# Attention keys ordered by column, values stored once per row range and loaded once per four tiles, q and keys in one request each

## The chip, the cores and the metric

The kernel runs on one NeuronCore of one Trainium2 chip. The metric is the device time of one execution in microseconds (us); smaller is better. Engines are called as in the profile: PE (TensorE), PEld (its weight loads), DVE (VectorE), ACT (ScalarE), POOL (GpSimd) and SP (SyncE, which here only issues DMA requests). DMA requests are issued by SP and by ACT, and sixteen DMA engines move the bytes.

## The reference, cut to what matters

One layer over 2048 latent tokens (a grid of 32 rows by 64 columns) and 256 context tokens, model width 1024, in f32. A combined projection feeds two head groups; the change touches the first, neighbourhood attention with 8 heads of width 64.

```
h_lat = rmsnorm(x) * (1 + scale) + shift ;  h_ctx likewise
na_q, na_k, na_v, na_g, r_q, r_k, r_v, r_g = split(h @ w_in)
# group A: each query reads an 8 x 16 window of the grid and all 256 context keys, in one softmax
s_loc = q . k[window] * 64**-0.5 + bias ;  s_ctx = q . k_ctx * 64**-0.5
p = softmax(concat(s_loc, s_ctx)) ;  o_na = p_loc @ v[window] + p_ctx @ v_ctx
# group B: retention in chunks of 128, forward and backward (r_q, r_k, r_v)
y = concat(o_na * silu(na_g), headnorm(o_ret) * silu(r_g)) @ w_out
out = rmsnorm(x + gate * y)
```

## The kernel before, in words

**Stages.** The projection comes first: the normed inputs are split into a high and a low f32r part, and every product is made of three matmuls (high by high, low by high, high by low). Projected q, k, v and gates go to DRAM (`qS`, `kS`, `vS`, `gS` and others). Then comes attention over 128 tiles, with further projection work woven in between as filler for PE (`fill`). The retention scans and the output projection end the program.

**Storing values.** `u_v` makes the values of 256 tokens and two head pairs into a tile `o` (a ring of two buffers) and stores it with one request on ACT's queue into `vS`, which is ordered by token. `jobs` lists the units of the projection in order; after each unit `tick` issues the stores that were put off by one unit, and `spill_step` issues one request of 512 KB on SP (`hS`).

**Attention tiles.** Head `h` has 16 tiles: four row ranges `i` by four column ranges `j`. A tile has 128 queries (8 rows by 16 columns). `KWIN[i]` gives the rows of its keys, (first, count), `CWIN[j]` the columns:

```
KWIN = [(0, 12), (4, 16), (12, 16), (20, 12)]
CWIN = [(0, 24), (8, 32), (24, 32), (40, 24)]
```

So a tile has 288, 384 or 512 grid keys and 256 context keys. The loop over `t` runs these steps, each some tiles behind the one before: `s_mm` (line 748) multiplies q by the grid keys, read straight out of the head's key tile `k2`, and by the context keys; `s_min`, `s_exp` and `s_norm` make the softmax on DVE, ACT and POOL; `p_tr` transposes the probabilities in groups of keys; `pv` (line 796) multiplies them by the values `vt`; `combine` adds the parts. The order of instructions on each engine is the order in which this loop writes them, so PE does nothing else while an `s_mm` waits for its q.

**Loads in attention.** All are on SP's queue, in program order. `load_head` brings a head's keys with two requests (high and low half of `k2`, 64 partitions each), and the context values `vc`; it runs at tile (1, 2) of the head before. `load_q` brings the queries of a row range with two requests of the same 64 rows, one to each half of the partitions; the ring `q` has two buffers, and the load for row range `i + 1` is issued at tile (i, 0), four tiles ahead. `load_v` brings four grid rows of values with four requests, one per column range, into a ring of six. `bias` brings a tile's bias (`nb`), `load_gate` a gate (`gt`). Each DMA request of SP or ACT takes the next of eight completion counters (DMAHW0 to DMAHW7 in the instruction lists), in turn, and waits until the last request on the same counter has landed.

Of the kernel before, what the change touches and what calls it, by code (L numbers as in the profile page):

```python
# [9 lines left out]
F32 = mybir.dt.float32  # L10
# [8 lines left out]
P = 128  # L19
D = 1024  # L20
KC = D // P
L = 2048
# [58 lines left out]
def hybrid_kernel(ctx: ExitStack, tc: tile.TileContext, a: dict, out: bass.AP):  # L81
# [63 lines left out]
    def store(dst, src, n=1):  # L145
        q = env["queue"]
        defer(n, lambda: q.dma_start(dst, src))
# [268 lines left out]
    def u_v(w, c0, tp):  # L416
        pm = yield from tokform(w, tp)
        vt = op.tile([P, 2, 2, 2, P], F32R, name="o")
        pv = pm.rearrange("p (t h e d) -> p t h e d", t=2, h=2, e=2)
        for e in range(2):  # L420
            hs, ls = slice(64 * e, 64 * e + 64), slice(64 - 64 * e, 128 - 64 * e)
            nc.scalar.copy(vt[:, :, :, e, hs], pv[:, :, :, e, :])
            nc.vector.tensor_tensor(vt[:, :, :, e, ls], pv[:, :, :, e, :], f(vt)[:, :, :, e, hs], ALU.subtract)
        store(vS[(c0 - 1024) // WG][tp * 256:(tp + 1) * 256].rearrange("(t p) h d -> p t (h d)", p=P),
              f(vt).rearrange("p t h e d -> p t (h e d)"))
# [279 lines left out]

    def load_head(h):
        k2 = kp.tile([P, LT], F32R, name="k2")
        for hl in range(2):
            nc.sync.dma_start(f(k2)[64 * hl:64 * hl + 64, :], kS[h // 2][64 * (h % 2):64 * (h % 2) + 64, hl, :])
        vh = vS[h // 4][:, h % 4, :]  # L710
        vc = kp.tile([P, 2, P], F32R, name="vc")
        nc.sync.dma_start(f(vc), vh[L:, :].rearrange("(n p) d -> p n d", p=P))
        return dict(k2=k2, vh=vh, vc=vc, vt={}, q={})

    def load_q(hd, h, i):
        q = kp.tile([P, 2, 512], F32R, name="q", bufs=2)
        src = qS[h // 2][i, 64 * (h % 2):64 * (h % 2) + 64]
        for e in range(2):
            nc.sync.dma_start(f(q)[64 * e:64 * e + 64], src)
        hd["q"][i] = q  # L720

    def load_v(hd, gs):
        for g in gs:
            vt = kp.tile([P, 4, P], F32R, name="vt", bufs=6)
            src = hd["vh"][4 * g * GW:(4 * g + 4) * GW, :].rearrange("(r c) d -> r c d", c=GW)
            for j, (c0, cw) in enumerate(CWIN):
                nc.sync.dma_start(f(vt)[:4 * cw, j, :], src[:, c0:c0 + cw, :])
            hd["vt"][g] = vt

    def bias(h, rt, ct):  # L730
        n, o = BT[rt][ct]
# [8 lines left out]
    def s_mm(t):  # L740
        h, i, j, kr0, kr, kc0, cw = dims(t)
        hd, nk, odd = heads[h], kr * cw, t % 2
        pl = sS[:, 1024:1024 + nk] if odd else sS[:, 512 - nk:512]
        pc = sS[:, 768:1024] if odd else sS[:, 512:768]
        kg = hd["k2"][:, :L].rearrange("p (r c) -> p r c", c=GW)
        for o, k in ((pl, kg[:, kr0:kr0 + kr, kc0:kc0 + cw]), (pc, hd["k2"][:, L:])):
            for hl in range(2):
                nc.tensor.matmul(o, hd["q"][i][:, hl, j * P:(j + 1) * P], k, start=(hl == 0), stop=(hl == 1))  # L748
        tl_st[t] = dict(s=sS[:, 768:1024 + nk] if odd else sS[:, 512 - nk:768], nk=nk, lo=LC * odd, co=nk * (1 - odd),
                        sp=ap_.tile([P, 768], F32, name="sp", bufs=3), st=ap_.tile([P, 4], F32, name="stt", bufs=4))  # L750
# [19 lines left out]
    def p_tr(t):  # L770
        h, i, j, kr0, kr, kc0, cw = dims(t)
        T = tl_st[t]
        sp, nk, ng_, cn = T["sp"], T["nk"], kr // 4, 4 * cw
# [13 lines left out]
    def pv(t):  # L787
        h, i, j, kr0, kr, kc0, cw = dims(t)
        T, hd = tl_st[t], heads[h]
        pt, ng_ = T["pt"], T["ng"]  # L790
        if t % 2 == 0:
            tl_st["po"] = psc.tile([P, 2, 2, P], F32, name="po")
        po = tl_st["po"]
        cn = 4 * cw
        for g in range(ng_):
            nc.tensor.matmul(po[:, t % 2, :, :], hd["vt"][kr0 // 4 + g][:cn, j, :], pt[:cn, g, :, :], start=(g == 0), stop=False)  # L796
# [37 lines left out]

    heads[0] = load_head(0)
    load_q(heads[0], 0, 0)
    load_v(heads[0], (0, 1, 2))
    for n in range(4):
        run(n)
        if n == 0:  # L840
# [116 lines left out]
    for t in range(NT + 3):  # L957
# [34 lines left out]
            load_gate(t)  # L992
        if i < 3 and j == 0:
            load_q(hd, h, i + 1)
        for g in {(0, 2): (3,), (0, 3): (4,), (1, 1): (5,), (1, 3): (6,), (2, 3): (7,)}.get((i, j), ()):
            load_v(hd, (g,))
        if h + 1 < NH:
            if i == 1 and j == 2:
                heads[h + 1] = load_head(h + 1)
            if i == 3:  # L1000
                nh = heads[h + 1]
                if j == 0:
                    load_q(nh, h + 1, 0)
                    bias(h + 1, 0, 0)
                    load_v(nh, (0,))
                if j == 2:
                    bias(h + 1, 0, 1)
                if j == 3:
                    bias(h + 1, 0, 2)
                    load_v(nh, (1, 2))  # L1010
# [295 lines left out]
def _bias_rows(rpb):  # L1306
# [4 lines left out]
    out = []  # L1311
    for i in (0, 1, 3):
        r = qr + 8 * i
        k = np.arange(KWIN[i][1]).reshape(1, -1, 1) + KWIN[i][0]
        lo = np.clip(r - 4, 0, GROWS - 8)
        for j in (0, 1, 3):
            c = qc + 16 * j
            m = np.arange(CWIN[j][1]).reshape(1, 1, -1) + CWIN[j][0]
# [27 lines left out]
```

## Time and profile before

| | |
|---|---|
| time of the three runs shown | 1433.92 us median (1433.7 to 1440.09) |
| the profiled execution | 1431.96 us, span 1430.0 us |
| PE busy | 1351.1 us, 94% of the span |
| DVE, ACT, POOL busy | 641.0, 531.0, 495.0 us |
| TensorE clock granted, mean | 0.986 |
| bytes moved by DMA | 264.14 MB |
| first and last `s_mm` matmul | 561.4 and 1072.9 us from the span's start |

Rows of the view by groups read "line engine operation, tile written <- tiles read, shape, count, then busy us, mean ns of one, idle time before them and what ended it". Waits read "who waited <- for whom: us in total, times, longest". Rows of stretches give each engine's busy us, the granted clock, the mean busy share of the sixteen DMA engines and GB/s. Of a DMA request, size and count are shown; the little packets of 4 bytes by which DMA engines report that they have finished are counted under "under 512 B".

### The profile page before, as it was taken

The page shows a single profiled execution, that of the slowest core. Times are in us where ns is not written, and L with a number is a line of the kernel's source. Part 1 is how long each engine was busy: PE and PEld are TensorE (multiplying, and loading weights), DVE is VectorE, ACT ScalarE, POOL GpSimd, SP SyncE. Part 2 cuts the span into 40 slices and gives each one's busy share as a digit, 9 for nine tenths or more (in the row PEclk, how much of TensorE's full clock was granted, in tenths as well). Part 3 has the DMA queues.
Part 4 walks back from the last instruction along what each step waited for, and adds up shares of the span by engine and source line. Part 5 has one row for each costly group of instructions (what it writes and reads, how often), then busy time and mean ns, then how long its engine had stood idle before and what let it go on. Part 6 is the DMA issues. An engine that isn't in the chain of part 4 may idle for free.

```text
span 1430.0 us, 22693 instructions
## 1 busy us (share of the span) xinstructions
PE 1351.1 (94%) x8380; PEld 1179.9 (83%) x8380; DVE 641.0 (45%) x1244; ACT 531.0 (37%) x1155; POOL 495.0 (35%) x499
## 2 busy tenths in 40 slices
PE   7989999999999999999899978798999989999997
PEld 2567899988887888998799877697999779888886
DVE  5786111100021222566666765476564544344445
ACT  5454212212212222655455433345563234333332
POOL 5442302202201221355354432235443144454442
PEclk9999999999999999999999998899999999999999
DMA  9444656223354677767758696867645998555433
GB/s 320 153 162 148 229 196 229 104 88 103 104 169 147 222 259 218 179 179 194 178 160 205 174 236 163 235 172 197 166 138 170 275 316 259 192 177 169 155 119 125
DMA packets 213072, 264.14 MB, mean 185 GB/s; under 512 B 14305, under 2 KB 160865, under 8 KB 211938
## 3 DMA queue, kind: packets, MB, share of 16 engines
q1 hardware_dynamic: 177282, 197.93, 48.1%
q10 hardware_dynamic: 35680, 64.76, 12.7%
q8 instruction: 67, 1.10, 0.3%
q14 instruction: 43, 0.35, 0.1%
HBM read 179.80 MB, written 82.84 MB: 184 GB/s over the span
## 4 chain that ended last, share of the span: by engine, by line
PE 73%; DMA 13%; DVE 7%; issue 2%; ACT 2%; POOL 2%; SPq 1%; ACTq 0%; DVEq 0%; POOLq 0%
PE mm L355 25%; PE mm L366 18%; PE mm L1190 10%; DMA q<-qS 5%; PE sS L748 4%; PE tr L775 2%; PE po L796 2%; DMA vt<-vS 2%; PE mm L915 2%; PE mm L299 2%; PE tr L777 1%; PE po L798 1%; DMA v<-rvS 1%; PE mm L1102 1%; PE mm L1101 1%
## 5 line engine op out<-in xcount | busy, mean ns | idle before, releaser
L355 PE MATMUL mm<-hhi,whi 128*128 128x512 f32 x640 | 260.0, 406 | 0.0
L355 PE MATMUL mm<-hlo,whi 128*128 128x512 f32 x640 | 254.0, 397 | 5.6 <-DVE hlo L268 2.2
L355 PE MATMUL mm<-hhi,wlo 128*128 128x512 f32 x640 | 253.8, 397 | 0.3 <-DVE wlo L336 0.3
L366 PE MATMUL mm<-whi,hhi 128*128 128x256 f32 x768 | 225.0, 293 | 0.0
L366 PE MATMUL mm<-wlo,hhi 128*128 128x256 f32 x768 | 217.3, 283 | 2.6 <-POOL wlo L336 2.6
L366 PE MATMUL mm<-whi,hlo 128*128 128x256 f32 x768 | 216.3, 282 | 0.0
L336 POOL TENSOR_TENSOR wlo<-st,whi 128x256 fp32r<-128x256 f32 (+1 forms) x97 | 112.3, 1175 | 251.1 <-ACT whi L334 250.8
L779 ACT CAST pt<-tr 128x640 fp32r<-128x640 f32 (+1 forms) x128 | 95.6, 747 | 217.9 <-PE tr L777 192.6
L785 DVE TENSOR_TENSOR pt<-tr,pt 128x640 fp32r<-128x640 f32 (+1 forms) x128 | 113.9, 890 | 105.2 <-ACT pt L779 104.6
L768 POOL TENSOR_SCALAR sp<-sp,stt 128x640 f32<-128x640 f32 (+2 forms) x128 | 103.7, 811 | 136.0 <-DVE stt L767 94.9
L366 PEld LDWEIGHTS mm<-wlo,hhi 128*128 128x128 f32 x768 | 145.4, 189 | 3.3 <-POOL wlo L336 3.2
L355 PEld LDWEIGHTS mm<-hlo,whi 128*128 128x128 f32 x640 | 121.0, 189 | 31.4 <-issue 3.2
L366 PEld LDWEIGHTS mm<-whi,hlo 128*128 128x128 f32 x768 | 145.7, 190 | 0.0
L366 PEld LDWEIGHTS mm<-whi,hhi 128*128 128x128 f32 x768 | 145.7, 190 | 0.0
L355 PEld LDWEIGHTS mm<-hhi,wlo 128*128 128x128 f32 x640 | 120.7, 189 | 29.5 <-DVE wlo L336 0.7
L355 PEld LDWEIGHTS mm<-hhi,whi 128*128 128x128 f32 x640 | 121.0, 189 | 28.5 <-issue 4.6
L757 DVE CUSTOM_DVE_ANT_0 sp<-sS,nb 128x640 f32<-128x640 f32 (+2 forms) x128 | 105.6, 825 | 53.4 <-PE sS L748 43.0
L748 PE MATMUL sS<-k,q 128*128 128x256 f32 (+3 forms) x512 | 101.7, 321 | 27.3 <-DMA q<-qS 21.8
L748 PEld LDWEIGHTS sS<-k,q 128*128 128x128 f32 x512 | 85.1, 192 | 36.5 <-issue 19.9
L762 ACT ACTIVATE sp<-sp,stt 128x640 f32<-128x640 f32 (+2 forms) x128 | 107.5, 839 | 20.1 <-DVE stt L757 19.8
L1190 PE MATMUL mm<-wor,y 128*128 128x512 f32 x384 | 95.6, 398 | 1.3 <-DVE xt L1199 1.2
L1190 PE MATMUL mm<-won,y 128*128 128x512 f32 x336 | 89.9, 406 | 0.0
(214 smaller groups left out, 2238.8 us busy)
## 6 DMA issues: line engine op xcount, KB each, us to landing
st<-in_w_in_dram SPq DMA_DIRECT2D x48, 512.0 KB
q<-qS SPq DMA_DIRECT2D x64, 256.0 KB
vS<-o ACTq DMA_DIRECT2D x18, 512.0 KB
k<-kS SPq DMA_DIRECT2D x16, 576.0 KB
kS<-o SPq DMA_DIRECT2D x16, 512.0 KB
woS<-g ACTq DMA_DIRECT2D x32, 256.0 KB
qS<-o ACTq DMA_DIRECT2D x16, 512.0 KB
vt<-vS SPq DMA_DIRECT2D x128, 64.0 KB
```

The source lines that it names most:

```text
L299: nc.tensor.matmul(aps[u][0:s.shape[2], :], s[:, 2 * j + k, :], w, start=(j == 0 and i == 0 and k == 0), stop=(j == 3 and i + 1 == len(ops ...
L336: eng.tensor_tensor(l, r, f(h), ALU.subtract)
L355: nc.tensor.matmul(pm[:, :n], ww[:, k, cs], h[:, k, :], start=(k == 0 and i == 0), stop=(k == KC - 1 and i == 2))
L366: nc.tensor.matmul(pm[:, t * WG:(t + 1) * WG], h[:, k, o:o + P], ww[:, k, :], start=(k == 0 and i == 0), stop=(k == KC - 1 and i == 2))
L748: nc.tensor.matmul(o, hd["q"][i][:, hl, j * P:(j + 1) * P], k, start=(hl == 0), stop=(hl == 1))
L757: nc.vector.tensor_tensor_reduce(T["sp"][:, :n], T["s"], nbz[big][:, o:o + n], -1.0, 3e38, ALU.add, ALU.min, T["st"][:, 0:1])
L762: nc.scalar.activation(sp[:, :n], sp[:, :n], AF.Exp, bias=st[:, 0:1], scale=-1.0, accum_out=st[:, 1:2])
L768: nc.gpsimd.tensor_scalar(sp[:, :n], sp[:, :n], st[:, 2:3], 0.0, ALU.mult, ALU.add)
L775: nc.tensor.transpose(tr[:cn, g, :], sp[:, T["lo"] + g * cn:T["lo"] + (g + 1) * cn], ident)
L779: nc.scalar.copy(pt[:, :ng_ + 2, 0, :], tr[:, :ng_ + 2, :])
L785: nc.vector.tensor_tensor(pt[:, :n, 1, :], tr[:, :n, :], f(pt)[:, :n, 0, :], ALU.subtract)
L1190: nc.tensor.matmul(pm, yy[:, k, :], ww[:, k, sl], start=(k == 0 and i == 0), stop=(k == 3 and i == 2))
```

## The change

Keys of a tile are taken column by column instead of row by row (`"p r c -> p c r"` in `s_mm`, and the same in the table of biases), so a transposed group is 8 columns by all rows of the row range, instead of 4 rows by all columns of the column range. Group sizes stay 96 or 128, and the number of groups over a head stays the same. The values of grid tokens are stored to `vB`, one tensor per row range with the partition order (column in a block of 8, row), so that one request of 96 or 128 partitions by 8 blocks brings what all four tiles of a row range need. A row that lies in two row ranges is stored twice; each store is one row of 64 tokens, on SP's queue. `load_q` and `load_head` make one request each, with the two halves as the outermost dimension of the DRAM side. Bias loads move one tile later. The two value jobs stand apart in `jobs`, a gate job between them.

```
-    vS = [dram.tile([LT, 4, P], F32, name=f"vS{t}") for t in range(2)]
+    vS = [dram.tile([LC, 4, P], F32, name=f"vS{t}") for t in range(2)]
+    vB = [[dram.tile([P, 8, 4 * P], F32, name=f"vB{t}_{i}") for i in range(4)] for t in range(2)]
...
+        if tp == 8:
+            store(vS[s].rearrange("(t p) h d -> p t (h d)", p=P), o)
+            return
+        for r in range(4 * tp, 4 * tp + 4):
+            for i, (kr0, kr) in enumerate(KWIN):
+                if kr0 <= r < kr0 + kr:
+                    dst = vB[s][i][:8 * kr].rearrange("(c r) b d -> r b c d", r=kr)[r - kr0]
+                    defer(1, lambda dst=dst, src=o[64 * (r % 2):64 * (r % 2) + 64, r % 4 // 2, :]: nc.sync.dma_start(dst, src))
...
-    jobs = [(1024, [(u_v, (tp,)) for tp in range(9)]), (1280, [(u_v, (tp,)) for tp in range(9)])]
-    jobs += [(c0, [(u_gate, (ct, b)) for ct in range(2) for b in range(4)]) for c0 in (1536, 1792)]
+    jobs = []
+    for e in range(2):
+        jobs += [(1024 + 256 * e, [(u_v, (tp,)) for tp in range(9)]), (1536 + 256 * e, [(u_gate, (ct, b)) for ct in range(2) for b in range(4)])]
...
-        for hl in range(2):
-            nc.sync.dma_start(f(k2)[64 * hl:64 * hl + 64, :], kS[h // 2][64 * (h % 2):64 * (h % 2) + 64, hl, :])
+        nc.sync.dma_start(f(k2), kS[h // 2][64 * (h % 2):64 * (h % 2) + 64].rearrange("p e t -> e p t"))
...
-        for e in range(2):
-            nc.sync.dma_start(f(q)[64 * e:64 * e + 64], src)
+        nc.sync.dma_start(f(q).rearrange("p e t -> p (e t)"), src.rearrange("p e t -> p (e t)").unsqueeze(0).to_broadcast([2, 64, 1024]))
...
-    def load_v(hd, gs):
-        for g in gs:
-            vt = kp.tile([P, 4, P], F32R, name="vt", bufs=6)
-            src = hd["vh"][4 * g * GW:(4 * g + 4) * GW, :].rearrange("(r c) d -> r c d", c=GW)
-            for j, (c0, cw) in enumerate(CWIN):
-                nc.sync.dma_start(f(vt)[:4 * cw, j, :], src[:, c0:c0 + cw, :])
-            hd["vt"][g] = vt
+    def load_v(h, i):
+        vt, n = kp.tile([P, 8, P], F32R, name="vt", bufs=3), 8 * KWIN[i][1]
+        nc.sync.dma_start(f(vt)[:n], vB[h // 4][i][:n, :, (h % 4) * P:(h % 4 + 1) * P])
+        heads[h]["vt"][i] = vt
...
-        for o, k in ((pl, kg[:, kr0:kr0 + kr, kc0:kc0 + cw]), (pc, hd["k2"][:, L:])):
+        for o, k in ((pl, kg[:, kr0:kr0 + kr, kc0:kc0 + cw].rearrange("p r c -> p c r")), (pc, hd["k2"][:, L:])):
...
-        for g in {(0, 2): (3,), (0, 3): (4,), (1, 1): (5,), (1, 3): (6,), (2, 3): (7,)}.get((i, j), ()):
-            load_v(hd, (g,))
+        if j == 3 and 3 < t < NT - 8:
+            load_v((t + 8) // 16, (t + 8) // 4 % 4)
```

What SP issues from tile (1, 2) of head 0 on, when the keys of head 1 are fetched (k, vc), before the change; `q` is the load for row range 3 of head 0, and the numbers behind a name only tell buffers apart:

```order
L709 DMA k_4452<-kS_61 64x2304 [waits DMAHW7_49]
L709 DMA k_4452<-kS_61 64x2304 [waits DMAHW0_49]
L712 DMA vc<-vS_65 128x2x128 [waits DMAHW1_49]
L727 DMA vt<-vS_65 96x1x128 [waits DMAHW3_49,PE_49]
L727 DMA vt<-vS_65 128x1x128 [waits DMAHW5_49]
L727 DMA vt<-vS_65 128x1x128 [waits DMAHW6_49]
L727 DMA vt<-vS_65 96x1x128 [waits DMAHW7_49]
L732 DMA nb_3984<-in_rpb_t_dram 128x288 [waits DMAHW0_49,DVE_49]
L719 DMA q<-qS_57 64x1024 [waits DMAHW1_49,PE_49]
L719 DMA q<-qS_57 64x1024 [waits DMAHW2_49]
```

The same place after the change:

```order
L717 DMA k_4531<-kS_61 128x1x2304 [waits DMAHW6_49]
L719 DMA vc<-vS_65 128x2x128 [waits DMAHW7_49]
L730 DMA vt<-vB_3_70 96x8x128 [waits DMAHW0_49,PE_49]
L735 DMA nb_4088<-in_rpb_t_dram 128x288 [waits DMAHW1_49,DVE_49]
L725 DMA q<-qS_57 128x1x1024 [waits DMAHW2_49,PE_49]
L735 DMA nb_4088<-in_rpb_t_dram 128x384 [waits DMAHW3_49,DVE_49]
L812 DMA gt<-gS_75 64x512 [waits DMAHW4_49,Pool_49]
L735 DMA nb_4088<-in_rpb_t_dram 128x288 [waits DMAHW6_49,DVE_49]
```

Two requests for keys, two for queries and four for values have become one each. The last `nb` of this piece uses the counter of `k` (DMAHW6), so it is issued when `k` has landed; `q` stands ahead of it.

One head later, again on SP after the change, the keys of head 2 and then the queries for row range 3 of head 1:

```order
L717 DMA k_5296<-kS_62 128x1x2304 [waits DMAHW3_49]
L719 DMA vc<-vS_65 128x2x128 [waits DMAHW4_49]
L730 DMA vt<-vB_3_70 96x8x128 [waits DMAHW6_49,PE_49]
L404 DMA rot<-in_rot_c_dram 128x512 [waits DMAHW7_49,DVE_49]
L404 DMA rot<-in_rot_s_dram 128x512 [waits DMAHW1_49,DVE_49]
L735 DMA nb_4088<-in_rpb_t_dram 128x288 [waits DMAHW2_49]
L725 DMA q<-qS_57 128x1x1024 [waits DMAHW3_49,PE_49]
```

Here `q` itself has come onto the counter of `k` (DMAHW3), since fewer requests lie between them.

In the projection, SP before the change issues only the spills and weight loads at the first value job (`st` is the raw weights):

```order
L173 DMA st<-in_w_in_dram 128x4x256 x2
L527 DMA hS_0_85<-hhi 128x1024 x4
L527 DMA hS_1_86<-hlo 128x1024 x4
L527 DMA hS_0_87<-hhi 128x1024
L173 DMA st<-in_w_in_dram 128x4x256 x2
```

After the change the stores of rows lie between the spills:

```order
L174 DMA st<-in_w_in_dram 128x4x256 x2
L433 DMA vB_0_67<-o 8x8x512 x4
L536 DMA hS_0_93<-hhi 128x1024
L433 DMA vB_0_67<-o 8x8x512
L433 DMA vB_1_68<-o 8x8x512
```

The 16 stores of grid values have left ACT's queue, and 112 row stores stand on SP's.

More of the change, by code (lines that the diff above doesn't have):

```diff
@@ L423, in u_v @@
             nc.vector.tensor_tensor(vt[:, :, :, e, ls], pv[:, :, :, e, :], f(vt)[:, :, :, e, hs], ALU.subtract)
-        store(vS[(c0 - 1024) // WG][tp * 256:(tp + 1) * 256].rearrange("(t p) h d -> p t (h d)", p=P),
-              f(vt).rearrange("p t h e d -> p t (h e d)"))
+        s, o = (c0 - 1024) // WG, f(vt).rearrange("p t h e d -> p t (h e d)")
+        if tp == 8:
[6 more added lines that the diff above has]
+                    defer(1, lambda dst=dst, src=o[64 * (r % 2):64 * (r % 2) + 64, r % 4 // 2, :]: nc.sync.dma_start(dst, src))
     def put_tok(dstt, c0, tp, r, n=1):
@@ L707, in load_head @@
         k2 = kp.tile([P, LT], F32R, name="k2")
-        for hl in range(2):
-            nc.sync.dma_start(f(k2)[64 * hl:64 * hl + 64, :], kS[h // 2][64 * (h % 2):64 * (h % 2) + 64, hl, :])
-        vh = vS[h // 4][:, h % 4, :]
+        nc.sync.dma_start(f(k2), kS[h // 2][64 * (h % 2):64 * (h % 2) + 64].rearrange("p e t -> e p t"))
         vc = kp.tile([P, 2, P], F32R, name="vc")
-        nc.sync.dma_start(f(vc), vh[L:, :].rearrange("(n p) d -> p n d", p=P))
-        return dict(k2=k2, vh=vh, vc=vc, vt={}, q={})
+        nc.sync.dma_start(f(vc), vS[h // 4][:, h % 4, :].rearrange("(n p) d -> p n d", p=P))
+        return dict(k2=k2, vc=vc, vt={}, q={})
     def load_q(hd, h, i):
@@ L772, in p_tr @@
         T = tl_st[t]
-        sp, nk, ng_, cn = T["sp"], T["nk"], kr // 4, 4 * cw
+        sp, nk, ng_, cn = T["sp"], T["nk"], cw // 8, 8 * kr
         for g in range(ng_):
@@ L793, in pv @@
         po = tl_st["po"]
-        cn = 4 * cw
+        cn = 8 * kr
         for g in range(ng_):
-            nc.tensor.matmul(po[:, t % 2, :, :], hd["vt"][kr0 // 4 + g][:cn, j, :], pt[:cn, g, :, :], start=(g == 0), stop=False)
+            nc.tensor.matmul(po[:, t % 2, :, :], hd["vt"][i][:cn, kc0 // 8 + g, :], pt[:cn, g, :, :], start=(g == 0), stop=False)
         for g in range(2):
@@ L836, in hybrid_kernel @@
     load_q(heads[0], 0, 0)
-    load_v(heads[0], (0, 1, 2))
+    for i in range(3):
+        load_v(0, i)
     for n in range(4):
@@ L1003, in hybrid_kernel @@
                     load_q(nh, h + 1, 0)
+                if j == 1:
                     bias(h + 1, 0, 0)
-                    load_v(nh, (0,))
-                if j == 2:
+                if j == 3:
                     bias(h + 1, 0, 1)
-                if j == 3:
-                    bias(h + 1, 0, 2)
-                    load_v(nh, (1, 2))
+        if h > 0 and (i, j) == (0, 0):
+            bias(h, 0, 2)
     def load_y(lo, kind, t):
@@ L1313, in _bias_rows @@
         r = qr + 8 * i
-        k = np.arange(KWIN[i][1]).reshape(1, -1, 1) + KWIN[i][0]
+        k = np.arange(KWIN[i][1]).reshape(1, 1, -1) + KWIN[i][0]
         lo = np.clip(r - 4, 0, GROWS - 8)
@@ L1317, in _bias_rows @@
             c = qc + 16 * j
-            m = np.arange(CWIN[j][1]).reshape(1, 1, -1) + CWIN[j][0]
+            m = np.arange(CWIN[j][1]).reshape(1, -1, 1) + CWIN[j][0]
             lc = np.clip(c - 8, 0, GW - 16)
```

## The prediction

> **What bounds the kernel now.** I read the page first, then who waits for whom on PE, then the stretches, then the DMA views.
>
> ```profile
> span 1430.0 us, 22693 instructions
> PE 1351.1 (94%) x8380; PEld 1179.9 (83%) x8380; DVE 641.0 (45%) x1244; ACT 531.0 (37%) x1155; POOL 495.0 (35%) x499
> DMA packets 213072, 264.14 MB, mean 185 GB/s; under 512 B 14305, under 2 KB 160865, under 8 KB 211938
> ```
>
> PE is the bound: 79 us of the span are all that it is not busy. Where those lie, and what the attention stage (first to last tile, 561 to 1085 us) looks like as a whole:
>
> ```profile
> PE sS L748 <- DMA q<-qS: 21.8, 7, 6.6
> PE mm L299 <- ACT o L286: 9.7, 1, 9.7
> PE po L796 <- DMA vt<-vS: 7.0, 2, 3.9
> ...
> PE sS L748 <- DMA vt<-vS: 1.0, 1, 1.0
> ```
>
> ```profile
> core 0: us, PE busy (x) PEld busy (x) DVE busy (x) ACT busy (x) POOL busy (x), PEclk, DMA share, GB/s
> 200.00:220.00 20.00, 20.00 (x171) 20.00 (x170) 3.07 (x8) 4.12 (x9) 0.38 (x1) 1.00 0.27 100
> 561.00:1085.00 524.00, 481.73 (x3551) 454.53 (x3550) 324.95 (x726) 261.48 (x546) 218.86 (x247) 0.97 0.69 182
> 1160.00:1180.00 20.00, 20.00 (x103) 16.75 (x102) 6.67 (x12) 7.40 (x18) 12.85 (x18) 1.00 1.08 346
> ```
>
> In attention PE idles 42 us of 524, 30 of them for q and values, and the clock is 0.97. That is all that quicker loads could bring. A row range (four tiles) takes 524/32 = 16.4 us now, 481.73/32 = 15.1 us of it PE work. The DMA engines are at 0.69 of their time there: transfers, not PE, are what the change moves, so the question is how each new request is carried.
>
> **How a request is spread.** The requests and their sizes (KB each), and a stretch just before attention in which value requests alone move data:
>
> ```profile
> st<-in_w_in_dram SPq DMA_DIRECT2D x48, 512.0 KB
> q<-qS SPq DMA_DIRECT2D x64, 256.0 KB
> ...
> k<-kS SPq DMA_DIRECT2D x16, 576.0 KB
> ...
> qS<-o ACTq DMA_DIRECT2D x16, 512.0 KB
> vt<-vS SPq DMA_DIRECT2D x128, 64.0 KB
> ...
> vt<-vS SPq DMA_DIRECT2D x128, 48.0 KB
> ...
> rg<-in_ret_g_t_dram SPq DMA_DIRECT2D x1, 2.0 KB
> ```
>
> ```profile
> DMA  1222322111000000000011113211223322222111
> GB/s 47 64 70 82 94 82 64 41 47 29 18 12 0 0 0 0 0 0 0 23 47 47 47 41 94 88 47 59 76 82 88 94 76 88 82 70 59 59 53 41
> DMA packets 355, 0.18 MB, mean 50 GB/s; under 512 B 12, under 2 KB 355, under 8 KB 355
> ```
>
> The second fence is 549 to 552.5 us: six requests are issued, all packets are those of 512 B of `vt`, and the DMA share never passes 3 tenths; 94 GB/s is the most. An ordinary stretch (543 to 553 us, with qS stores in it) reaches 9 tenths and 430 GB/s:
>
> ```profile
> DMA  7998989799854423999992101210000122222179
> GB/s 145 221 203 213 295 213 262 279 397 430 330 205 172 152 94 133 389 424 387 426 393 82 55 29 59 86 53 29 0 0 8 45 74 61 82 84 72 49 297 360
> ```
>
> So `vt` runs on about a quarter of the engines. What is special about it is its DRAM side: four grid rows outermost (`src[:, c0:c0+cw]`, 4 x cw x 128), where the others have 64 or more outermost. The completion packets agree. The listing of issues (65 groups, the first and the last shown above) sums to 1,039 requests; at 16 reports each that is 16,624, but the page has only 14,305 packets under 512 B in all. 256 `vt` requests with 4 reports instead of 16 are 3,072 fewer, 13,552, which fits; in the short stretch there are 12 small packets, three finished requests at 4.
>
> I therefore take it that a request runs on as many engines as its outermost count allows. The new `load_q` has `to_broadcast([2, 64, 1024])` and the new `load_head` has `"p e t -> e p t"`: two outermost. Both then run on two engines, where two requests of 64 rows ran on sixteen.
>
> [...]
>
> **The change, part by part.**
>
> *q and keys on two engines.* Rate of one engine: 430/16 = 26.9 GB/s at the peak above, 94/4 = 23.5 in the `vt` stretch, 346/(16 x 1.08) = 20.0 in the row 1160 to 1180 with all engines loaded. I take 25.2, between the first two, since only two engines will be loaded and the rest lightly. Bytes in the stage: 182 GB/s x 524 us = 95.4 MB. Of these q is 31 x 512 KB = 16.3 MB, k is 7 x 1152 KB = 8.3 MB, and 70.9 MB are other requests. After the change each of the two engines carries half of q and k, 12.3 MB, and a sixteenth of the rest, 4.4 MB: 16.7 MB, which at 25.2 GB/s takes 662 us (621 at 26.9, 834 at 20.0). The stage cannot be shorter than that, and it is 524 now.
>
> In one head: a q takes 262 KB/25.2 = 10.4 us, the keys 590 KB/25.2 = 23.4 us, the others 4.4 MB/25.2/32 = 5.5 us a row range. In an ordinary row range q is issued at its start and lands at the fixed time + 10.4 + most of 5.5, about 17 us later: just longer than the 15.1 us of PE work. The keys are issued in the middle of row range 1 and stand ahead of the q for range 3, so range 2 lasts until both are through, about 40 us: `s_mm` of tile (3, 0) should wait some 25 us in seven heads. The fixed time shows at the program's start:
>
> ```profile
> 0.72 0.41 SPq L455 DMA_DIRECT2D silc<-in_c_dram  x1
> 2.42 0.21 ACT L456 ACTIVATE silc<-silc 128x16 f32<-128x16 f32 x1 [0.42 <-DMA silc<-in_c_dram]
> ```
>
> 8 KB are there 1.7 us after issue. In the three ordinary ranges of each head nothing of q is queued for that time: 24 x 1.7 = 41 us (0 if other requests fill it all). Stage: 662 + 41 = 703 us.
>
> *The first head.* Keys are asked for at 530.5 us and the first `s_mm` runs at 561.4:
>
> ```profile
> L709 SPq DMA_DIRECT2D k<-kS x16: 480/592/1285, 530.5 to 978.7; - x16
> L748 PE MATMUL sS<-k,q x512: 274/291/660, 561.4 to 1072.9; 128*128 128x256 f32 x86, 128*128 128x384 f32 x44, 128*128 128x512 f32 x21, 128*128 128x288 f32 x20
> ```
>
> 530.5 + 1.7 + 23.4 + 10.4 + 1.7 = 567.7, and up to six qS stores on the same engines, 33 KB or 1.3 us each, make 575: 7 to 14 us late, I take 10.
>
> *Values loaded once.* 256 requests become 32, of 96 or 128 outermost on both sides, the same bytes on all engines; the two `vt` waits (7.0 and 1.0 us) go, and 224 issues leave SP. The ring of three gives each load eight tiles. None of it shortens a stage that q sets: 0. What SP saves was not on the path either:
>
> ```profile
> L727 SPq DMA_DIRECT2D vt<-vS x256: 504/616/1790, 543.5 to 1059.2; - x128
> SPq L727 <- DMA vt<-vS: 22.7, 30, 2.5
> ```
>
> The second line shows SP waiting on completion counters; with q and k late, those waits grow (rival below).
>
> *Values stored by rows.* 112 requests of 128 KB on SP instead of 16 of 512 KB on ACT, 14.7 MB instead of 8.4. A unit of the value job is 48 matmuls at 293 ns, 14 us, and issues up to 8 stores at about 0.6 us (the SP row above), 5 us; `o` has two buffers, so a store has some 14 us to land. The row 200 to 220 has PE at 20.00 of 20 and DMA at 0.27, so this stays covered: 0, at most one late unit in sixteen jobs, 5 us. Its outermost 8 should mean 8 engines, enough for 16 KB each. The price of a matmul is in
>
> ```profile
> L366 PE MATMUL mm<-whi,hhi 128*128 128x256 f32 x768 | 225.0, 293 | 0.0
> L748 PE MATMUL sS<-k,q 128*128 128x384 f32 x128 | 35.0, 355 | 17.1 <-DMA q<-qS 13.3 <-DVE stt L757 1.8 <-DMA vt<-vS 1.0
> L748 PE MATMUL sS<-k,q 128*128 128x512 f32 x64 | 21.4, 416 | 1.0 <-DVE stt L757 0.9
> L748 PE MATMUL sS<-k,q 128*128 128x288 f32 x64 | 14.5, 308 | 9.2 <-DMA q<-qS 8.5 <-DVE stt L757 0.7
> ```
>
> *Keys by column.* The grid-key matmuls (last three rows, 70.9 us) now read elements 64 apart. No row shows such a read by PE; its cost is between 0 and a doubling, 70.9 us. PE work in the stage would be 552.6 us at the worst, below 703, so q covers it: 0 here. Transposes and `pv` keep their counts, and the softmax its sizes: 0. The later biases spare SP waits for DVE: 0.
>
> **Sum**, against the profiled execution's 1432 us (2 us under the median): 1432 - 524 + 703 + 10 = 1621 us.
>
> **The rivals.**
>
> *Everything behind the keys stops.* A request waits for its completion counter, eight requests back; in the third instruction list the q for range 3 waits for the keys' own counter, and ACT's stores take counters too. Then q starts only when the keys have landed, and up to one range of PE work a head, 15.1 us, is no longer covered: 7 x 15.1 = 106 us more, 1727. For it: three requests fewer lie between k and q. Against it: in the head before, q goes out first.
>
> *The loads are quick enough.* The requests are spread over sixteen engines after all, or two are faster than any row shows; then the 30 us of waits and part of the low clock go: I take 24 us off, 1408, faster than before. It decides when two engines do 16.7 MB in the 482 us of PE work, 35 GB/s each, or when the split is four or more. Against it: the peak of 26.9 and the quarter share of `vt`.
>
> *Spread well, but PE pays for the stride.* 1408 + 71 = 1479, slower; it needs the split to be good and a doubled read. [...]
>
> **How the numbers follow.** Two engines carry q and keys, as summed: 0.78, by its bounds 1529 (26.9 GB/s, no gaps, nothing late at the start) to 1795 (20.0 GB/s). Stopped behind the keys: 0.12, inside that range. Quick loads: 0.05. Stride alone: 0.03. No change within 0.5%, which is about what can be measured: 0.02. Faster 0.05, same 0.02, slower 0.93. The range is that of the first two cases, 1525 to 1795.
>
> **What would show it.** PE's wait for `q<-qS` grows from 21.8 us to about 200, its longest from 6.6 to 20 or more, once in each of seven heads at tile (3, 0); packets under 512 B fall below 16 a request; the DMA share of the stage falls from 0.69 to about 0.5 while PE waits; waits for `vt` vanish; the projection before 530 us keeps its time. I am wrong if the wait for q falls, or if `sS` matmuls lengthen and the stage does not.

## The result, and the profile after

The changed kernel takes 1676.17 us (median of 4 runs, 1674.84 to 1681.17) against 1433.81 us (4 runs, 1430.14 to 1440.09) on the same chip: a ratio of 1.169, 95% interval 1.164 to 1.174. The forecast was 1621, range 1525 to 1795, slower.

The page after, in the lines that were shown of before: span, busy time, packets.

```profile
span 1673.0 us, 22622 instructions
PE 1435.6 (86%) x8380; PEld 1216.5 (73%) x8380; DVE 643.3 (38%) x1244; ACT 531.9 (32%) x1155; POOL 494.1 (30%) x499
DMA packets 215072, 270.43 MB, mean 162 GB/s; under 512 B 13233, under 2 KB 159793, under 8 KB 213938
```

PE does the same 8380 matmuls, is busy 84 us longer and idle 237 us instead of 79. The requests (KB each) and who waits for whom on PE (us in total, times, longest):

```profile
q<-qS SPq DMA_DIRECT2D x32, 512.0 KB
vB<-o SPq DMA_DIRECT2D x112, 128.0 KB
k<-kS SPq DMA_DIRECT2D x8, 1152.0 KB
...
vt<-vB SPq DMA_DIRECT2D x16, 512.0 KB
```

```profile
PE sS L751 <- DMA q<-qS: 116.5, 8, 25.5
PE tr L778 <- DVE pt L788: 52.3, 4, 20.0
PE sS L751 <- DVE stt L760: 18.1, 6, 7.0
PE mm L300 <- ACT o L287: 11.1, 1, 11.1
PE mm L356 <- ACT whi L335: 8.9, 1, 8.9
```

The wait for `q` has grown from 21.8 to 116.5 us and none for `vt` is left on PE. Two others are new: transposes that wait for the softmax (`pt`), 52.3 us, and 8.9 us in the projection (L356). Stretch by stretch, cut at the first score matmul (587.1 us; it was at 561.4) and at 1326, where before has 1085:

```profile
0.00:587.00 587.00, 541.78 (x2844) 439.95 (x2844) 155.94 (x236) 153.00 (x239) 133.88 (x94) 0.98 0.53 178
587.00:1326.00 739.00, 561.43 (x3557) 487.83 (x3558) 328.83 (x727) 262.48 (x547) 220.72 (x248) 0.86 0.42 131
1326.00:1673.00 347.00, 332.40 (x1981) 288.76 (x1980) 158.55 (x281) 116.47 (x369) 139.51 (x158) 0.98 0.63 199
```

The projection is 26 us longer (587 for 561), attention 215 (739 for 524), the rest 2: the 243 us between the spans. In attention the DMA engines are busy 0.42 of their time, 0.69 before, and the granted clock is 0.86. A stretch of attention in 40 slices, 812 to 850 us:

```profile
DMA  1127111110111011152016889711138911114699
GB/s 33 52 99 254 56 63 47 50 69 39 47 58 67 39 58 58 58 144 89 36 42 144 258 222 302 184 61 52 52 91 265 249 55 52 49 46 105 190 325 310
```

For long runs of slices one tenth of the engines is busy and some 50 GB/s move, which reads as two engines of sixteen at 25 GB/s each; in 21.7 of the 38 us the trace has exactly two packets under way. In these slices the keys, and then a `q`, are on their way, and next to nothing else moves.

### The profile page after: what moved, and what is told of

Its sections match the earlier page's. It is cut to its first block, busy times and chain, and to the rows that moved or that the text cites. A ratio compares the mean times of both kernels' runs of the same rounds, so it can differ in the third digit from the quotient of the medians.

```text
span 1673.0 us, 22622 instructions
## 1 busy us (share of the span) xinstructions
PE 1435.6 (86%) x8380; PEld 1216.5 (73%) x8380; DVE 643.3 (38%) x1244; ACT 531.9 (32%) x1155; POOL 494.1 (30%) x499
## 2 busy tenths in 40 slices
DMA packets 215072, 270.43 MB, mean 162 GB/s; under 512 B 13233, under 2 KB 159793, under 8 KB 213938
## 4 chain that ended last, share of the span: by engine, by line
PE 61%; DMA 22%; SPq 7%; DVE 4%; issue 3%; POOL 1%; ACT 1%; ACTq 0%; DVEq 0%; POOLq 0%
PE mm L356 21%; PE mm L367 13%; PE mm L1194 9%; DMA q<-qS 7%; PE sS L751 5%; DMA k<-kS 5%; SPq L735 4%; DMA nb<-in_rpb_t_dram 4%; SPq L730 2%; PE tr L778 2%; PE po L799 2%; DMA vt<-vB 2%; PE mm L919 2%; DMA st<-in_w_in_dram 1%; PE mm L300 1%
## 5 line engine op out<-in xcount | busy, mean ns | idle before, releaser
L751 PE MATMUL sS<-k,q 128*128 128x256 f32 (+3 forms) x512 | 166.0, 461 | 134.6 <-DMA q<-qS 116.5
L356 PE MATMUL mm<-hhi,whi 128*128 128x512 f32 x640 | 263.5, 412 | 8.9 <-ACT whi L335 8.9
L356 PE MATMUL mm<-hlo,whi 128*128 128x512 f32 x640 | 257.0, 402 | 3.9 <-DVE hlo L269 2.2
L356 PE MATMUL mm<-hhi,wlo 128*128 128x512 f32 x640 | 256.5, 401 | 2.9 <-POOL wlo L337 2.9
L751 PEld LDWEIGHTS sS<-k,q 128*128 128x128 f32 x512 | 100.8, 214 | 191.5 <-issue 163.9
L367 PE MATMUL mm<-whi,hhi 128*128 128x256 f32 x768 | 229.4, 299 | 2.1 <-DVE o L386 2.1
L367 PEld LDWEIGHTS mm<-whi,hhi 128*128 128x128 f32 x768 | 149.8, 195 | 2.4 <-DVE o L386 2.4
L367 PEld LDWEIGHTS mm<-wlo,hhi 128*128 128x128 f32 x768 | 149.2, 194 | 2.5 <-POOL wlo L337 2.5
L356 PEld LDWEIGHTS mm<-hhi,whi 128*128 128x128 f32 x640 | 122.9, 192 | 38.0 <-ACT whi L335 10.0
L367 PEld LDWEIGHTS mm<-whi,hlo 128*128 128x128 f32 x768 | 149.9, 195 | 0.0
L356 PEld LDWEIGHTS mm<-hhi,wlo 128*128 128x128 f32 x640 | 122.7, 192 | 33.4 <-POOL wlo L337 4.0
L356 PEld LDWEIGHTS mm<-hlo,whi 128*128 128x128 f32 x640 | 122.9, 192 | 29.7 <-issue 3.2
L778 PE MATMUL tr<-ident,sp 128*128 128x128 f32 (+1 forms) x448 | 75.4, 288 | 52.3 <-DVE pt L788 52.3
L765 ACT ACTIVATE sp<-sp,stt 128x640 f32<-128x640 f32 (+2 forms) x128 | 109.0, 852 | 24.1 <-DVE stt L760 23.9
L778 PEld LDWEIGHTS tr<-ident,sp 128*128 128x128 f32 (+1 forms) x448 | 56.1, 141 | 60.1 <-issue 50.2
```

The lines of the kernel that those rows point to most:

```text
L356: nc.tensor.matmul(pm[:, :n], ww[:, k, cs], h[:, k, :], start=(k == 0 and i == 0), stop=(k == KC - 1 and i == 2))
L367: nc.tensor.matmul(pm[:, t * WG:(t + 1) * WG], h[:, k, o:o + P], ww[:, k, :], start=(k == 0 and i == 0), stop=(k == KC - 1 and i == 2))
L765: nc.scalar.activation(sp[:, :n], sp[:, :n], AF.Exp, bias=st[:, 0:1], scale=-1.0, accum_out=st[:, 1:2])
```

## The experiments

Each is timed against the kernel before on the same chip (1427 to 1431 us there); times are medians.

### Which request costs what

Both requests in halves of 64 rows again, all else as changed:

```diff
-        nc.sync.dma_start(f(k2), kS[...].rearrange("p e t -> e p t"))
+        for hl in range(2):
+            nc.sync.dma_start(f(k2)[64 * hl:64 * hl + 64, :], kS[...][:, hl, :])
...
-        nc.sync.dma_start(f(q)..., src....unsqueeze(0).to_broadcast([2, 64, 1024]))
+        for e in range(2):
+            nc.sync.dma_start(f(q)[64 * e:64 * e + 64], src)
```

> The changed kernel, but q and keys with two requests of 64 rows each again (all else of the change stays). Theory A, two DMA engines: the wait of sS for q was nearly all of the loss; it falls from 116 us to under 25, what stays is the strided read of the keys by PE (about +62 us of busy time in the grid-key matmuls, 70.9 to 132.9) and about 12 us in the value jobs: 1470 to 1495 us. Rival B, the value loads and stores on SP's queue (vt waiting for PE ahead of q, eight completion counters): splitting the requests puts more of them on the same queue and counters, so the time stays at 1640 to 1700. Rival C, PE itself (stride and low clock): the stage keeps most of its length, 1600 or more.

1456.51 us, ratio 1.020 (1.017 to 1.023): 220 us of the loss are gone, and 29 are left. That is theory A, some 14 us better than its range. Only the keys split (first half of that diff), so that `q` alone is on two engines:

> The changed kernel with two requests for the keys, q still one request. Theory A: 31 q of 10.2 us each on two engines and no keys ahead of them; a row range needs about 17 us for q and about 17 us of PE work with the stride, so most is covered: 1490 to 1540. If each request costs in proportion to its bytes on the two engines (q 16.3 of 24.5 MB), q alone would keep two thirds of the loss, about 1590 to 1620.

1555.77 us, 1.090 (1.085 to 1.094). Only `q` split, so that the keys alone are:

> The changed kernel with two requests for q, the keys still one request. Theory A: keys hold two engines for 22 us, everything issued behind them waits for its share on these two, but the first q needed behind them comes about 25 us later, so the wait is short: 1480 to 1530. If the keys alone made the long waits (7 x 25 us), they stay: 1600 to 1660.

1539.10 us, 1.078 (1.072 to 1.084). Both times fall between the two cases that had been written down. So `q` on two engines costs 99 us and the keys 83, and both together 220, 38 more than the two. An estimate of why stands with the stage's sum below.

### One request, 64 rows outermost

Is it the number of requests, or what stands outermost? One request each, as in the change, but with the 64 rows outermost:

```diff
-        ... kS[...].rearrange("p e t -> e p t"))
+        ... kS[...].rearrange("p e t -> (p e) t"))
-        ... src....unsqueeze(0).to_broadcast([2, 64, 1024]))
+        ... src....unsqueeze(1).to_broadcast([64, 2, 1024]))
```

> The changed kernel with one request each for q and keys, but the 64 rows outermost and the two halves inside (partition 2 c + e instead of 64 e + c, on both sides, so the products are the same). The number of requests is that of the change. Theory A: outermost 64 and 128 run on sixteen engines: as e1 or some us below, 1465 to 1490. If it is the number, size or order of the requests that hurts, it stays near 1676.

1459.85 us, 1.022 (1.019 to 1.025), 5 us under theory A's range: the same as two requests, so the number of requests is not the cause. What differs is the number of engines, and the small packets by which engines report count it. The page of this run, which has the same requests as the changed kernel:

```profile
DMA packets 215632, 270.43 MB, mean 185 GB/s; under 512 B 13793, under 2 KB 160353, under 8 KB 214498
```

The changed kernel has 13233 packets under 512 B, 560 fewer: 14 for each of its 40 loads of `q` and keys, as it must be if two engines report where sixteen did.

### The two loads alone, in the kernel before

The one-request loads with 64 rows outermost, put into the kernel before, with none of the rest of the change:

> The kernel before with only this: one request each for q and keys, 64 rows outermost as in e4. 40 requests fewer, the same bytes on sixteen engines. Theory: the waits for q (22 us) come from the many value requests and their counters, so they shrink by a third at most: 1410 to 1428. Rival: they come from the two-request form of q and go altogether: 1395 to 1405.

1412.27 us, 0.990 (0.988 to 0.992); PE's wait for `q` falls from 21.8 to 9.0 us. The time is in the theory's range, but the wait shrank by more than the third that it allowed. The idea of one request was good for 1%. And the two-outermost loads of the change put into the kernel before:

> The kernel before with only the changed requests for q and keys (two halves outermost). Keys row by row, values as before. The sum of the prediction without the stride: 1621, within 1590 to 1660, below the changed kernel by 20 to 60 us, if what lies between 1621 and 1676 is PE work with the stride. Rival: values on four engines, two of them the same two, and 256 requests more on the counters make it as slow as the changed kernel or slower, 1680 to 1760.

1756.3 us, 1.231 (1.229 to 1.234), 80 us slower than the changed kernel itself: the rival, and not the prediction's sum. Its packets, its longest waits on PE, and the waits of ACT and PE for values:

```profile
DMA packets 211872, 264.13 MB, mean 151 GB/s; under 512 B 13105, under 2 KB 159665, under 8 KB 210738
```

```profile
PE sS L746 <- DMA q<-qS: 123.0, 19, 14.4
PE tr L773 <- DVE pt L783: 117.4, 14, 24.9
...
ACT pt L777 <- DMA vt<-vS: 73.3, 4, 30.5
...
PE po L794 <- DMA vt<-vS: 27.9, 2, 18.8
```

The small packets are 1200 fewer than the 14305 of before: 80 loads at 16 reports have become 40 at 2. The 256 small value loads on four engines now land late, and PE (27.9 us) and ACT (73.3 us) wait for them, and PE for the softmax behind ACT (117.4 us). The rest of the change, the single value load above all, is worth some 80 us in that company, where the waits for values before had been 8. The run does not part the value load from the other edits. An estimate says that it is enough: 14.7 MB of values on four engines instead of sixteen put 2.75 MB more on each of the four, 117 us at the 23.5 GB/s of the prediction's `vt` stretch. From the first to the last score matmul this run takes 97 us longer than the changed kernel (822 for 725):

```profile
L746 PE MATMUL sS<-k,q x512: 274/295/689, 574.7 to 1396.5; 128*128 128x256 f32 x86, 128*128 128x384 f32 x44, 128*128 128x512 f32 x21, 128*128 128x288 f32 x20
```

```profile
L751 PE MATMUL sS<-k,q x512: 277/448/802, 587.1 to 1312.2; 128*128 128x256 f32 x86, 128*128 128x384 f32 x44, 128*128 128x512 f32 x21, 128*128 128x288 f32 x20
```

It needs two of the four engines to be those of `q` and keys, which no row here shows.

### Keys in runs of eight

What are the 29 us that stay when `q` and keys run on sixteen engines? The score matmul reads keys 64 elements apart. The version with 64 rows outermost, with the keys in runs of eight neighbours (rows of a block of eight columns), bias and stored values in the same order:

```diff
-        ... kg[...].rearrange("p r c -> p c r")
+        ... kg[...].rearrange("p r (g c) -> p g r c", c=8)
-                    dst = vB[s][i][:8 * kr].rearrange("(c r) b d -> r b c d", r=kr)[r - kr0]
+                    dst = vB[s][i][:8 * kr].rearrange("(r c) b d -> r b c d", r=kr)[r - kr0]
```

> As e4 (q and keys in one request each, 64 rows outermost), and the keys of a tile in groups of 8 columns, inside a group row by row, so PE reads runs of 8 elements instead of single ones 64 apart; the values are stored in the same order and still loaded once per four tiles. Theory A (the stride doubles the grid-key matmuls and is fully exposed once q is on time): those matmuls return to 70.9 us and the time falls by about 60 us from e4, to 1390 to 1410. Rival: a run of 8 is too short to be read at full speed, or the stride only showed as busy time: 1430 to 1460.

1405.75 us, 0.985 (0.983 to 0.987): 54 us faster than the same kernel by column, and faster than before. The grid-key matmuls by form (busy us, mean ns of one), by column in the changed kernel first, then one of them by column with 64 rows outermost, then in runs of eight:

```profile
L751 PE MATMUL sS<-k,q 128*128 128x384 f32 x128 | 65.3, 605 | 31.6 <-DVE stt L760 17.7 <-DMA q<-qS 13.9
...
L751 PE MATMUL sS<-k,q 128*128 128x512 f32 x64 | 41.2, 740 | 0.0
L751 PE MATMUL sS<-k,q 128*128 128x288 f32 x64 | 26.4, 509 | 103.0 <-DMA q<-qS 102.6 <-DVE stt L760 0.4
```

```profile
L751 PE MATMUL sS<-k,q 128*128 128x384 f32 x128 | 64.4, 599 | 0.8 <-DVE stt L760 0.8
```

```profile
L751 PE MATMUL sS<-k,q 128*128 128x384 f32 x128 | 36.3, 367 | 1.9 <-DVE stt L760 1.8
L751 PE MATMUL sS<-k,q 128*128 128x512 f32 x64 | 22.3, 432 | 0.7 <-DVE stt L760 0.7
L751 PE MATMUL sS<-k,q 128*128 128x288 f32 x64 | 14.8, 314 | 0.9 <-DVE stt L760 0.9
```

The first fence is the changed kernel, 132.9 us in all; the third 73.4, near the 70.9 of before. The second shows that the late loads and the low clock have little part in it: 599 ns with a clock of 1.00 in the stage, 605 with 0.86. The long stride costs about 60 us of PE work, in the prediction's bound of 0 to 70.9. The doubling behind that bound was the author's assumption, which no row of before shows; the runs show 605 ns with single elements 64 apart, 367 with runs of eight and 355 with the neighbours of before (128x384). No run here tries another length of run.

Then the same order in the changed kernel with its two-engine requests:

> The changed kernel with its requests for queries and keys as they are (two outermost, two DMA engines), but the keys in runs of eight rows of one column block, so that a score matmul reads neighbouring keys. Theory: the stage is not wholly bounded by the two engines; part of what 1676 has above the forecast of 1621 is TensorE work at the large stride that lies after each late load, and the time is 1620 to 1650. Rival: the late loads cover all of that work and the time stays 1665 to 1680.

1669.76 us, 1.166 (1.161 to 1.171): 6 us less, and the two intervals overlap. The rival held. Under late loads 60 us of PE work cost next to nothing.

### The projection's 17 us

In that last fast version the first score matmul is still at 578.2 us, where before had 561.4, with `PE mm L356 <- ACT whi L335` in the list of waits. Are SP's row stores in the way of the weights? Store each row once in one tensor for a group of heads, 64 stores instead of 112:

```diff
-    vB = [[dram.tile([P, 8, 4 * P], ...) for i in range(4)] for t in range(2)]
+    vB = [dram.tile([8, 8 * GROWS, 4 * P], ...) for t in range(2)]
-            for i, (kr0, kr) in enumerate(KWIN):
-                if kr0 <= r < kr0 + kr:
-                    dst = vB[s][i][:8 * kr]....[r - kr0]
-                    defer(1, ...)
+            dst = vB[s][:, 8 * r:8 * r + 8, :]
+            defer(1, ...)
```

> As the version with keys in runs of eight rows and one-request loads with 64 rows outermost (1405.75 us), but a group of heads has one value tensor and each grid row's values are stored once: 64 stores on SyncE in place of 112. Theory: the PE's wait for the weights' high half in the projection (9.8 us in two waits there) comes because SyncE's row stores, at 0.6 to 0.9 us each and up to eight in a unit that takes TensorE about 5.6 us, hold back the weight loads queued behind them; with four stores in a unit that wait falls below 3 us and the time is 1389 to 1398. Rival: the weight loads are late for another reason (their buffers, their landing), the wait stays near 10 us and the time is 1402 to 1408.

1390.06 us, 0.971 (0.969 to 0.974), the fastest version here and 2.9% faster than before. The row stores of the changed kernel, then those of this version with its score matmuls (ns min/median/max, first and last start):

```profile
L433 SPq DMA_DIRECT2D vB<-o x112: 565/574/1824, 172.5 to 337.4; - x112
```

```profile
L431 SPq DMA_DIRECT2D vB<-o x64: 570/571/705, 172.8 to 321.8; - x64
...
L749 PE MATMUL sS<-k,q x512: 277/294/530, 560.6 to 1028.3; 128*128 128x256 f32 x86, 128*128 128x384 f32 x44, 128*128 128x512 f32 x21, 128*128 128x288 f32 x20
```

A single store now holds SP for 705 ns at most where it was 1824, the wait at L356 for `whi` is gone, and attention starts at 560.6 us again. The stores of one unit on SP (start, us, what), in the changed kernel and then here:

```profile
184.34 8.78 SPq L433 DMA_DIRECT2D vB<-o  x8
```

```profile
184.22 2.43 SPq L431 DMA_DIRECT2D vB<-o  x4
```

This run takes away bytes (8.4 MB instead of 14.7) as well as requests, so it does not part the two. The DMA engines as a whole were not busier, though: from 168 to 232 us their share is 0.62 before and 0.59 in the changed kernel, while PE's busy time falls from 63.34 to 55.07 us:

```profile
168.00:232.00 64.00, 63.34 (x534) 63.03 (x533) 8.51 (x20) 11.95 (x25) 12.53 (x6) 1.00 0.62 227
```

```profile
168.00:232.00 64.00, 55.07 (x457) 54.17 (x456) 7.64 (x18) 8.71 (x20) 4.21 (x3) 0.96 0.59 194
```

Moving the 112 stores to ACT instead (`nc.scalar.dma_start`, runs of eight) was the other try:

> As e5, with the row stores of the values issued by ACT instead of SP. Theory: the 9.4 us that PE waits at 224 us for whi (a weight load behind the row stores on SP) and 3 to 4 us at 345 us go: 10 to 14 us below e5, 1378 to 1398. Rival: the 112 issues at about 0.4 us hold up ACT, which evicts every product there, and the time does not fall or rises by some us.

1416.63 us, 0.994 (0.991 to 0.996), 11 us slower than with SP:

```profile
PE mm L356 <- ACT whi L335: 19.2, 2, 14.9
```

That is the rival again. ACT rounds the weights, and these stores stand ahead of that on its queue: the stall went with them.

### Keys behind the queries

The forecast was 55 us short. In the chain that ended last, the changed kernel has these steps (start, us, what):

```profile
882.21 39.37 DMA k<-kS
921.58 0.02 issue
921.59 0.02 SPq L725
921.61 0.03 issue
921.64 15.70 DMA q<-qS
937.34 0.14 issue
937.47 1.37 PE sS L751 x4
```

`q` is issued at the instant the keys have landed, as the order in the section on the change has it (its counter is that of the keys). Is it that order which costs? The keys are asked for later, behind the `q` of range 3:

```diff
-            if i == 1 and j == 2:
+            if i == 2 and j == 0:
                 heads[h + 1] = load_head(h + 1)
```

> The changed kernel with one edit: a head's keys are asked for at the start of row range 2, behind the queries of range 3, and no longer in the middle of row range 1, ahead of them. Bytes, requests and the two DMA engines are the same; SyncE's next load of queries no longer comes onto the completion counter of the keys while they are under way. Theory: the forecast of 1621 was short by about 55 us because the queries of range 3 start only when the keys have landed (38 us for the keys, then 15.7 for the queries, one after the other in the chain of waits), so that the two engines stand empty for some 5 us at each such place and PE waits about 28 us a head. With the queries queued behind the keys ahead of time, the wait of a head is 10.4 + 23.4 + 10.4 us plus other traffic of about 11 less two row ranges of 17.5 us, some 21 us, 7 less in seven heads: 1620 to 1645. Rival: the two engines are busy all through the stage and their rate was taken too high, the order is then indifferent: 1665 to 1685.

1686.55 us, 1.180 (1.175 to 1.184): 10 us slower. The theory failed. The rival, two engines that are busy all through so that the order is indifferent, came within 2 us of its range; the 10 us themselves are not explained. PE's waits say where the time went, with ACT's below them:

```profile
PE tr L778 <- DVE pt L788: 131.5, 7, 26.1
PE sS L751 <- DMA q<-qS: 37.1, 7, 12.6
```

```profile
ACT pt L782 <- DMA nb<-in_rpb_t_dram: 67.3, 3, 26.9
```

The wait for `q` fell from 116.5 to 37.1 as intended, and the wait for the softmax took its place, 131.5 for 52.3. How a late load reaches the softmax is seen in the changed kernel too; ACT at 624 to 651 us (start, us, what, idle before it):

```profile
625.34 0.19 ACT L765 ACTIVATION_READ_ACCUMULATOR sp<-sp,stt 128x1 f32 x1
649.20 0.38 ACTq L148 DMA_DIRECT2D rvS<-o  x1
649.68 0.80 ACT L782 CAST pt<-tr 128x768 fp32r<-128x768 f32 x1 [24.15 <-DMA vt<-vB]
```

The store `rvS` starts when a `vt` load has landed, whose data it does not use. What ties them is a completion counter that both use (DMAHW0 in the instruction list). The `vt` load is issued at 621.03 us and lands 28.09 us later. Of its 768 packets of 512 B, 672 start from 627.0 to 629.2 us; the other 96, two sixteenths of them, start with 32 of the `vc` load from 646.9 us on, when the keys' packets (623.5 to 647.2 us) end. So a piece of it stood behind the keys on two engines. ACT stands 24 us in front of a store that nothing waits for, with the cast that PE's transposes need behind it. In the run with the keys behind the queries the request at fault is a bias (`nb`).

## Why the prediction was right, and where it was not

**Two engines (the main step): right.** In these runs the number of engines went with the outermost count. The slices of 50 GB/s are two engines at 25, where 25.2 was taken; the version with 64 rows outermost gives back 216 us; and the small packets fall by 14 for each load. In the trace a head's keys take 23.2 to 26.6 us, with two of their packets under way in 20.8 to 22.9 of these; before, they took 6.5 to 9.0 us, with 10 to 13 under way on the mean. The prediction's own count was 753 short of the 14,305 that it was to fit, but 13,538 of these are packets of 4 bytes, for its 13,552. The same count for the changed kernel, with 2 reports for each of 40 loads of `q` and keys, 16 for each of 32 value loads and 8 for each of 112 row stores, is 12,480, and its trace has 12,466. One request with two outermost is slow (1676 us), and one with 64 outermost is fast (1460 us).

**The stage: 703 foreseen, 739 measured.** The bytes were right: 131 GB/s x 739 us = 96.8 MB, of which 24.6 are `q` and keys. The terms made of them were not. The row of the stage gives 16 x 0.42 x 739 = 4966 us of engine time. `q` and keys at 25.2 GB/s are 976 of these, 488 on each of the two engines. That leaves 3990 us for the other 72.2 MB, 249 on each of the sixteen, 18.1 GB/s an engine. So the two engines had 488 + 249 = 737 us of work in 739: by this estimate they were busy nearly all through. Two terms of the sum were mis-sized, in opposite directions. The other requests were priced at the pace of `q` and keys, 175 us in the 662, and took 249. The gaps, "24 x 1.7 = 41", are close to nothing: in the trace's packet records fewer than two packets are under way in only 30 of the 739 us, 11 of them before 1300 us. That the total missed by only 36 us here is in part luck. Packets overlap on an engine (the row of 1160 to 1180 us before has a share of 1.08), so the 249 may be a little high.

By the same sum `q` alone on two engines is 323 + 249 = 572 us and the keys alone 165 + 249 = 414, an estimate too. The stage takes 531 us with 64 rows outermost. So by these sums each alone hides much of its time under PE's work and both together do not: the estimate of why 220 is more than 99 + 83. It takes the two engines to be the same for both; in the first head `q` is issued at 553.4 us, and its packets run from 575.9 us, just when the keys' end (575.7). How the keys alone still cost 83 us is not shown.

It fits that the cheaper PE work (runs of eight) and the other order (keys behind the queries) brought next to nothing with two-engine loads. The late requests, behind `q` or keys, settle who waits: the list of what would show it had PE's wait for `q` at about 200 us, and it is 116.5, with 52.3 + 18.1 us of waits for the softmax. Of the other signs on that list, the small packets, the longest wait (25.5 us), the DMA share (0.42 for about 0.5) and the end of PE's waits for `vt` came out; ACT does wait for `vt`, 24.1 us at the cast. "The projection before 530 us keeps its time" failed, by 17 us (below). The upper end of the range, 1795, is 1793 by the terms that it names.

**Rival "everything behind the keys stops" (0.12, 1727):** its mechanism is there, in the chain of waits and on ACT, but not at its price of 106 us, and its remedy for `q` alone does not help. With two engines busy nearly all through, it moves the wait from one place to another.

**First head: +10 foreseen.** In the version with runs of eight, with sixteen engines, attention starts at 578.2 us; in the changed kernel at 587.1. So the keys and `q` on two engines cost 9 us there (5 against the version by column with 64 rows outermost, which starts at 582.2).

**Values stored by rows: 0, at most 5, foreseen; 17 measured** (578.2 against 560.6 us with each row stored once). The step that failed is "48 matmuls at 293 ns, 14 us". The durations of matmuls overlap: the row that the prediction itself quotes for 200 to 220 us has 171 of them in 20.00 us, 117 ns each, and 48 take 5.6 us. Eight stores were to take 5 us of SP's time under 14 us of PE work; they take up to 8.8 us, and PE needs 5.6. With spills and weight loads on the same queue SP falls behind (PE waits 8.9 us for `whi`, and not with four stores a unit). That part of the loss stays when everything else is mended.

**Values loaded once: 0 foreseen.** Not settled alone. The kernel before with the good loads takes 1412 us; with values once, each row stored once and runs of eight as well it takes 1390. Under two-engine loads the rest of the change, values loaded once above all, is worth some 80 us, by the run that puts those loads into the kernel before.

**Keys by column: 0 in this stage, as foreseen** (6 us, within error), and 54 us where the loads are good. "Spread well, but PE pays for the stride" was forecast at 1479, with the doubling that no row showed, and is the kernel with 64 rows outermost, 1460: the condition failed, not the mechanism. That the number is so near is luck: the stride costs 54 us of time and not 71, and the 17 us of the row stores, which it did not have, make up for it.

**Low clock: not foreseen.** From 921 to 938 us, when PE stands before `q`, the granted clock is 0.50:

```profile
921.00:938.00 17.00, 0.53 (x2) 0.56 (x3) 0.00 (x0) 0.00 (x0) 0.00 (x0) 0.50 0.39 128
```

In attention it is 0.86 on the mean, 0.97 before. In the version by column with 64 rows outermost, where PE waits for next to nothing there, it is 1.00:

```profile
582.00:1113.00 531.00, 528.25 (x3545) 456.33 (x3544) 327.06 (x725) 261.75 (x546) 220.31 (x247) 1.00 0.55 175
```

PE's busy time in the stage is 561.43 us in the changed kernel and 528.25 here, with the same strided reads; so 33 of the 80 us more than before (481.73) come with the late loads and the low clock. The score matmuls that nothing changed (128x256) go from 284 to 307 ns, but 296 of these are there at the clock of 1.00 too, next to the strided ones. What the low clock alone costs was not shown.

## What to carry to other kernels

Before merging requests, look at what stands outermost on both sides: one request with 64 outermost made the kernel 1% faster, one with two outermost made it 23% slower. Look for the cost of a request that is slow on a few engines at engines that never read its data: here a `vt` load landed 28 us after its issue, two sixteenths of it behind the keys, and ACT stood 24 us for its counter. To price such a load, add up all that its few engines carry, the other requests at their own pace (about 18 GB/s an engine here, by the estimate above, not 25). Take an engine's pace from a row of a window (171 matmuls in 20.00 us, 117 ns each), not from the mean duration of one (293 ns), before you let it cover a queue.

## What was not expected of the hardware

- A score matmul that reads its keys 64 elements apart took 605 ns in the changed kernel, where one that reads neighbours took 355 before (128x384), 740 for 416 (128x512), 509 for 308 (128x288); runs of eight took 367, 432 and 314.
- Two halves of 64 rows in two requests and one request with 64 outermost were equally fast in the changed kernel (1456.5 and 1459.9 us), but in the kernel before one request was 1% faster (1412.3 against 1427.1 us).
- `q` and the keys on two engines cost 220 us together, and 99 and 83 each alone.
- A store on ACT stood 24 us until a load on SP had landed, whose data it does not use, with the softmax's cast behind it.
